# Raw weight buffers of the feed-forward groups dealt out anew: block 22 with two of its own, blocks 11, 21 and 12 in a ring of four

## The chip, the cores and the metric

The kernel runs on one core of a Trainium2 chip. The metric is device time in microseconds (us). The five engines (TensorE for matmuls, VectorE or DVE, ScalarE or ACT, GpSimd or POOL, and SyncE or SP, which issues most transfers) each run their own list of instructions in order and wait for one another through semaphores.

## The reference

A two-layer decoder trunk in float32 on 528 columns (16 meta tokens and 512 tokens): a retention layer and a gated DeltaNet layer, each followed by a SwiGLU feed-forward block. What matters here is the feed-forward block, whose hidden width is 2816:

```python
def swiglu(h, w_gate, w_up, w_down):
    return (jax.nn.silu(h @ w_gate) * (h @ w_up)) @ w_down
...
    for i in range(DEPTH):
        ...
        h = h + mix
        h = h + swiglu(rmsnorm(h, ffn_norm_w[i]), ffn_w_gate[i], ffn_w_up[i], ffn_w_down[i])
```

## The kernel before, in words

**Precision.** Every float32 matmul is made of three: weights and data are each split into a high half (a cast on ScalarE) and a low half (a subtraction on VectorE), and `mm3` (L400 to L407) multiplies high by high, high by low and low by high. A *split* of a raw weight block of 128x1024 (`split_w`, L177) is thus one cast into `whi` (L397) and one subtraction into `wlo` (L398). `whi` and `wlo` have three buffers each, so a cast waits until the matmuls of the third product before have read their weights.

**Hidden half of a feed-forward block** (`ffn_hidden`, L890). The 22 pairs of gate and up tiles are handled two at a time: 11 groups in each layer. For each, `ffn_quad` (L334) fetches four raw blocks of 512 KB, named 11, 21, 22 and 12. The first two groups (`PLAIN`) are done plainly: one row of products with 11 and 12, one with 21 and 22. Beside them the *forms* of the data (`forms`, L191: b11, t1, t2, b22, t3, b21, t4, with their sums in a tile that is also called `wsum`) are made on VectorE and ScalarE. The other nine groups go through `strassen` (L342), which needs seven products of 24 matmuls where the plain way needs eight. In the order of the code they use:

- b11: block 11
- t1: s = 21 + 22 (L374, into the tile `wsum`, of which there is one)
- t2: s = s + 11 (L377)
- b22: s = s + 12 (L380)
- t3: 21 = 11 + 21, written over block 21 (L385)
- b21: block 12
- t4: block 22

Each is split and multiplied, and products add up in the accumulators x, z and y. Between them results are taken out: L364 copies x or z on ScalarE, L368 adds on VectorE, L955 to L961 make silu(gate) times up. The second L364 takes z out after t1, and b22 then adds to z. In layer 0 a matmul of these products has 264 columns, in layer 1 it has 256.

**Raw buffers.** `raw_w` (L174) deals out a ring of `RAW` = 4 buffers, `wraw`, which all weights of the kernel share. In `ffn_quad` blocks 11 and 12 take from that ring; 21 and 22 alternate in two buffers `sraw` of the stage's own pool. A transfer into a buffer waits until the last reader of what it held is done: of 11 that is L377 or L385, of 12 its split after L380, of 21 the split for t3, of 22 the split for t4, the last of the group. SP issues the transfers in its own order, so one that waits holds those behind it.

**The norm at a stage's start.** `row_rsqrt` (L475) sums squares with two kinds of small matmuls (L489, L491), takes the power on GpSimd (L497) and spreads the result with matmuls (L500, L504) in the middle of the first plain row.

**Who sets the order.** The code is written product by product. A list scheduler places the instructions on each engine when the program is built, by its own estimates of when buffers and data are ready, so another dealing of buffers also changes orders. On the chip the order is fixed.

Of the kernel before, what the change touches and what calls it, by code (L numbers as in the profile page):

```python
# [14 lines left out]
P = 128  # L15
# [35 lines left out]
class Hybrid:  # L51
# [282 lines left out]
    def ffn_quad(self, src, sp):  # L334

        raw = {}
        for i, n in enumerate(("11", "21", "22", "12")):
            raw[n] = self.raw_w() if n[0] == "1" else self.t(sp, [P, 1024], "sraw", bufs=2)
            self.nc.sync.dma_start(raw[n], src[i])
        return raw  # L340

# [1433 lines left out]
```

## Time and profile before

| what | us |
|---|---|
| median of 3 runs | 1740.63 (1739.11 to 1741.3) |
| the profiled execution's own time | 1740.59 |
| its span, first to last instruction | 1738.8 |
| TensorE waiting for `wlo` of L398 (all stages) | 5.5 in 13 waits |
| SP holding L339 for a split's subtraction L398 | 198.8 in 45 waits |
| SP holding L339 for L377 | 139.1 in 14 waits |
| layer 0, seven-product groups | 511.69 to 699.20 |
| layer 1, seven-product groups | 1413.71 to 1602.42 |

Times in views are microseconds from the span's start, mean durations of groups are ns. PE is TensorE's matmuls, PEld its weight loads, which run beside matmuls. The end of a matmul is modelled, so the distance from one matmul's start to the next says more than its busy time. "SPq" is SP's queue: a wait there costs nothing unless someone waits for the transfer. The chain of waits follows the work that ended last back to what released it.

### The profile page before, as it was taken

The numbers are of one execution on the slowest core, as the hardware profiler recorded it, in microseconds if no ns is written. First come the engines' busy times: TensorE is split into PE (matmuls) and PEld (weight loads), VectorE is DVE, ScalarE is ACT, GpSimd is POOL, SyncE is SP. The second block draws the span as 40 slices with busy tenths as digits, with TensorE's granted clock in tenths as the row PEclk, the third lists the DMA queues.
The fourth block names the chain that finished last, engine by engine and source line by source line (L and its number), as shares of the span: only waits on it lengthen the run. The fifth ranks groups of instructions, "written<-read, shape, count | busy, mean of one in ns | idle before, by whom it ended". The sixth has DMA issues, their size and how long they took to land.

```text
span 1738.8 us, 30404 instructions
## 1 busy us (share of the span) xinstructions
PE 1696.0 (98%) x12455; PEld 1577.0 (91%) x12455; DVE 1209.5 (70%) x1830; ACT 854.8 (49%) x1524; POOL 75.8 (4%) x130
## 2 busy tenths in 40 slices
PE   9999999899999999999999999999999999999997
PEld 9998989899999999999999978797977889999886
DVE  7868787873497777533688777685858797777322
ACT  5554454553354544422565537665656544445322
POOL 1000000000000000000030000010101000000010
PEclk9999999999999999999999999999999999999999
DMA  6333234472313332333264463332322233333321
GB/s 215 134 97 121 86 108 142 139 246 87 110 62 98 113 107 82 100 89 95 81 209 159 132 180 114 120 113 98 113 96 75 86 97 97 98 99 108 97 97 49
DMA packets 84524, 197.72 MB, mean 114 GB/s; under 512 B 19888, under 2 KB 37472, under 8 KB 83104
## 3 DMA queue, kind: packets, MB, share of 16 engines
q1 hardware_dynamic: 77056, 193.13, 34.2%
q10 hardware_dynamic: 6960, 1.84, 0.5%
q8 instruction: 98, 1.61, 0.4%
q0 software_dynamic: 368, 0.80, 0.1%
q14 instruction: 42, 0.34, 0.1%
HBM read 171.41 MB, written 24.33 MB: 113 GB/s over the span
## 4 chain that ended last, share of the span: by engine, by line
PE 72%; DVE 16%; ACT 5%; DMA 4%; issue 3%; POOL 1%; ACTq 0%; SPq 0%; DVEq 0%; POOLq 0%
PE g L407 53%; PE m L407 13%; DVE wlo L398 5%; ACT whi L397 3%; DMA sraw<-in_w_gu_dram 3%; DVE wraw L264 1%; DVE wsum L380 1%; DVE wsum L377 1%; DVE wsum L374 1%; DMA wraw<-in_w_ret_dram 1%; DVE xlo L530 1%; DVE wlo L171 1%; DVE xhi L398 1%; POOL ss L1435 0%; DMA xhi<-d_sg 0%
## 5 line engine op out<-in xcount | busy, mean ns | idle before, releaser
L171 DVE TENSOR_TENSOR wlo<-wraw,whi 128x1024 fp32r<-128x1024 f32 (+1 forms) x140 | 166.4, 1191 | 177.5 <-ACT whi L170 175.4
L170 ACT CAST whi<-wraw 128x1024 fp32r<-128x1024 f32 (+1 forms) x140 | 143.3, 1024 | 261.8 <-PE g L407 141.3
L407 PE MATMUL g<-fht,whi 128*128 128x264 f32 (+1 forms) x864 | 248.2, 287 | 13.2 <-ACT xlo L291 13.0
L407 PE MATMUL g<-xhi,whi 128*128 128x264 f32 (+1 forms) x1024 | 254.3, 313 | 0.1
L407 PE MATMUL g<-xhi,wlo 128*128 128x264 f32 (+1 forms) x1024 | 247.6, 306 | 2.0 <-DVE wlo L171 2.0
L407 PE MATMUL g<-xlo,whi 128*128 128x264 f32 (+1 forms) x1024 | 247.8, 306 | 0.3 <-DVE xlo L461 0.3
L407 PE MATMUL g<-fht,wlo 128*128 128x264 f32 (+1 forms) x864 | 245.6, 284 | 0.9 <-DVE wlo L398 0.8
L407 PE MATMUL g<-flt,whi 128*128 128x264 f32 (+1 forms) x864 | 245.3, 284 | 0.0
L407 PEld LDWEIGHTS g<-fht,whi 128*128 128x128 f32 x864 | 163.0, 189 | 14.0 <-ACT xlo L291 13.6
L407 PEld LDWEIGHTS g<-xhi,whi 128*128 128x128 f32 x1024 | 165.9, 189 | 10.7 <-issue 0.7
L407 PEld LDWEIGHTS g<-xhi,wlo 128*128 128x128 f32 x1024 | 165.9, 189 | 10.6 <-DVE wlo L171 2.2
L407 PEld LDWEIGHTS g<-xlo,whi 128*128 128x128 f32 x1024 | 166.2, 189 | 7.5 <-DVE xlo L461 0.7
L407 PEld LDWEIGHTS g<-fht,wlo 128*128 128x128 f32 x864 | 162.7, 188 | 1.7 <-DVE wlo L398 1.6
L407 PEld LDWEIGHTS g<-flt,whi 128*128 128x128 f32 x864 | 163.2, 189 | 0.0
L397 ACT CAST whi<-wraw 128x1024 fp32r<-128x1024 f32 x107 | 111.9, 1049 | 97.7 <-issue 36.6
L398 DVE TENSOR_TENSOR wlo<-wraw,whi 128x1024 fp32r<-128x1024 f32 x107 | 129.9, 1220 | 25.8 <-ACT whi L397 25.7
L407 PE MATMUL g<-fhb,wlo 128*128 128x264 f32 (+1 forms) x432 | 124.1, 287 | 4.8 <-DVE wlo L398 4.7
L407 PE MATMUL g<-fhb,whi 128*128 128x264 f32 (+1 forms) x432 | 123.2, 285 | 0.0
L407 PE MATMUL g<-flb,whi 128*128 128x264 f32 (+1 forms) x432 | 122.4, 283 | 0.0
L397 ACT CAST whi<-wsum 128x1024 fp32r<-128x1024 f32 x54 | 56.7, 1050 | 79.8 <-DVE wsum L377 46.7
L398 DVE TENSOR_TENSOR wlo<-wsum,whi 128x1024 fp32r<-128x1024 f32 x54 | 66.0, 1222 | 40.4 <-ACT whi L397 40.4
L407 PEld LDWEIGHTS g<-fhb,wlo 128*128 128x128 f32 x432 | 81.2, 188 | 7.5 <-DVE wlo L398 7.4
(454 smaller groups left out, 3955.6 us busy)
## 6 DMA issues: line engine op xcount, KB each, us to landing
wraw<-in_w_ret_dram SPq DMA_DIRECT2D x56, 512.0 KB, 3.4
wraw<-in_w_gu_dram SPq DMA_DIRECT2D x44, 512.0 KB, 3.4
sraw<-in_w_gu_dram SPq DMA_DIRECT2D x44, 512.0 KB, 3.4
wraw<-in_w_d_dram SPq DMA_DIRECT2D x38, 512.0 KB, 3.5
wraw<-in_w_ro_dram SPq DMA_DIRECT2D x16, 512.0 KB, 3.9
wraw<-in_w_dqk_dram SPq DMA_DIRECT2D x16, 512.0 KB, 3.3
wraw<-in_w_dv_dram SPq DMA_DIRECT2D x16, 512.0 KB, 3.6
wraw<-in_w_dg_dram SPq DMA_DIRECT2D x16, 512.0 KB, 3.4
```

Of the source, the lines that this page charges most:

```text
L170: nc.scalar.copy(hi[:, c], raw[:, c])
L171: nc.vector.tensor_tensor(lo[:, c], raw[:, c], hi[:, c].bitcast(F32), op=ALU.subtract)
L264: self.nc.vector.tensor_tensor(raw[dst], raw[dst], raw[src], op=ALU.add)
L374: nc.vector.tensor_tensor(s, raw["21"], raw["22"], op=ALU.add)
L377: nc.vector.tensor_tensor(s, s, raw["11"], op=ALU.add)
L380: nc.vector.tensor_tensor(s, s, raw["12"], op=ALU.add)
L397: self.nc.scalar.copy(hi, src)
L398: self.nc.vector.tensor_tensor(lo, src, hi.bitcast(F32), op=ALU.subtract)
L407: mm(o, l, r[which], start=first and n == 0, stop=last and n == 2, **kw)
L530: nc.vector.tensor_tensor(o, x, y, op=op)
```

## The change

```diff
         raw = {}
         for i, n in enumerate(("11", "21", "22", "12")):
-            raw[n] = self.raw_w() if n[0] == "1" else self.t(sp, [P, 1024], "sraw", bufs=2)
+            raw[n] = self.t(sp, [P, 1024], "sraw", bufs=2) if n == "22" else self.raw_w()
             self.nc.sync.dma_start(raw[n], src[i])
         return raw
```

The two `sraw` buffers now hold block 22 of two groups in turn. The ring of four holds 11, 21 and 12, so three of its buffers go to each group; block 21 of a group takes the buffer in which 11 of the group before stood. No transfer, cast, sum or product is added or left out.

The scheduler places the work of a seven-product group otherwise. On VectorE, in the second of the nine groups in layer 0, behind the split for b22 (`wsum_5813` and `5775`, `5779` are this group's sum and blocks 21 and 12; `wsum_6045`, `6005`, `6007`, `6009` the next group's sum and blocks 11, 21, 22):

```order
 L380 TENSOR_TENSOR wsum_5813<-wsum_5813,wraw_5779 128x1024
 L398 TENSOR_TENSOR wlo_5878<-wsum_5813,whi_5877 128x1024
-L398 TENSOR_TENSOR wlo_5912<-sraw_5775,whi_5911 128x1024
+L374 TENSOR_TENSOR wsum_6045<-wraw_6007,sraw_6009 128x1024
+L398 TENSOR_TENSOR wlo_5912<-wraw_5775,whi_5911 128x1024
+L385 TENSOR_TENSOR wraw_6007<-wraw_6005,wraw_6007 128x1024
 L398 TENSOR_TENSOR wlo_5943<-wraw_5779,whi_5942 128x1024
 L368 TENSOR_TENSOR ra_5905<-ra_5905,g_5782 128x528
```

The next group's L374 and L385 moved up among the splits of this one; before, they stood some nine instructions further on, behind the split of the next block 11.

On ScalarE, in the same group, from the copy of x after b11 (`ra_5843`) to the cast of block 12:

```order
 L364 COPY ra_5843<-g_5781 128x528
+L397 CAST whi_5877<-wsum_5813 128x1024
+L397 CAST whi_5911<-wraw_5775 128x1024
 L364 COPY ra_5874<-g_5782 128x528
-L397 CAST whi_5877<-wsum_5813 128x1024
-L397 CAST whi_5911<-sraw_5775 128x1024
 L397 CAST whi_5942<-wraw_5779 128x1024
```

The casts for b22 and t3 moved ahead of the copy of z.

SP's queue at the same place (11, 21, 22 and 12 of a group are 6005, 6007, 6009 and 6011; 5775 and 5777 are 21 and 22 of the group before, 6237 is 11 of the next):

```order
 L339 DMA wraw_6005<-in_w_gu_dram 128x1024
-L339 DMA sraw_5775<-in_w_gu_dram 128x1024
+L339 DMA sraw_6009<-in_w_gu_dram 128x1024
+L339 DMA wraw_6007<-in_w_gu_dram 128x1024
 L339 DMA wraw_6011<-in_w_gu_dram 128x1024
-L339 DMA sraw_5777<-in_w_gu_dram 128x1024
 L339 DMA wraw_6237<-in_w_gu_dram 128x1024
```

Before, 21 and 22 of a group came behind 11 of the next group and later; now a group's four blocks stand together, 22 ahead of 21.

At the start of layer 1's feed-forward block, in its first plain row, TensorE has this (`x` is the normed data, `am` and `acc` the sums of squares):

```order
 L407 MATMUL g_15338<-xlo_15067,whi_15330 128x512
 L407 MATMUL g_15338<-xhi_15066,wlo_15331 128x512
-L489 MATMUL m_15365<-ones_76,am_15354 96x1
-L491 MATMUL m_15365<-ones_76,acc_15068 128x1 x4
 L407 MATMUL g_15338<-xhi_15066,whi_15330 128x512
 L407 MATMUL g_15338<-xlo_15067,whi_15330 128x512
 L407 MATMUL g_15338<-xhi_15066,wlo_15331 128x512
+L489 MATMUL m_15365<-ones_76,am_15354 96x1
+L491 MATMUL m_15365<-ones_76,acc_15068 128x1 x4
```

The row-sum matmuls moved back by three matmuls; L500 and L504 keep their place. VectorE's order there, with the split of the first block 21 (`wlo_15420`):

```order
 L473 TENSOR_TENSOR acc_15068<-acc_15068,ra_15261 128x528
 L1510 TENSOR_TENSOR h_73<-h_73,g_15270 128x512 x2
+L398 TENSOR_TENSOR wlo_15420<-wraw_15324,whi_15419 128x1024
 L461 SCALAR_TENSOR_TENSOR xlo_15067<-h_73,ffnw_452,xhi_15066 128x528
 L473 TENSOR_TENSOR acc_15068<-acc_15068,ra_15298 128x528
```

Before, that subtraction stood behind the copy into `am` (L481), five instructions further on. In layer 0 the same split moved ahead of the last norm step, and TensorE's order is the same as before.

## The prediction

> **What bounds the kernel now.** I read the page first: the busy shares, then the chain that ended last.
>
> ```profile
> span 1738.8 us, 30404 instructions
> PE 1696.0 (98%) x12455; PEld 1577.0 (91%) x12455; DVE 1209.5 (70%) x1830; ACT 854.8 (49%) x1524; POOL 75.8 (4%) x130
> ...
> PE g L407 53%; PE m L407 13%; DVE wlo L398 5%; ACT whi L397 3%; DMA sraw<-in_w_gu_dram 3%; DVE wraw L264 1%; DVE wsum L380 1%; DVE wsum L377 1%; DVE wsum L374 1%; DMA wraw<-in_w_ret_dram 1%; DVE xlo L530 1%; DVE wlo L171 1%; DVE xhi L398 1%; POOL ss L1435 0%; DMA xhi<-d_sg 0%
> ```
>
> TensorE is the bound, so a change can give only what TensorE loses. But the chain has 3% (some 45 us) on transfers into `sraw`, the buffers that are dealt out anew. That is no 45 us to win: most of it lies beside matmuls. So next I cut both feed-forward stages into their nine seven-product groups, from the first matmul of one to that of the next. The columns are the stretch, its length, then the busy time and count of TensorE, its weight loads, VectorE, ScalarE and GpSimd, the clock and the DMA.
>
> ```profile
> 574.48:595.00 20.52, 20.52 (x171) 20.52 (x169) 16.44 (x20) 10.23 (x14) 0.00 (x0) 1.00 0.32 103
> ...
> 657.22:678.56 21.34, 20.88 (x170) 20.58 (x169) 17.19 (x21) 10.54 (x15) 0.00 (x0) 1.00 0.32 100
> ...
> sum 187.51, PE 186.02 PEld 184.82 DVE 148.44 ACT 92.73 POOL 0.00; mean PE 20.67 PEld 20.54 DVE 16.49 ACT 10.30 POOL 0.00
> ```
>
> ```profile
> 1413.71:1435.49 21.78, 20.67 (x169) 20.25 (x168) 18.37 (x23) 11.01 (x15) 0.00 (x0) 1.00 0.31 98
> 1435.49:1455.86 20.37, 20.37 (x170) 20.21 (x169) 16.03 (x19) 10.22 (x14) 0.00 (x0) 1.00 0.32 104
> ...
> sum 188.71, PE 184.57 PEld 182.11 DVE 149.39 ACT 92.42 POOL 0.00; mean PE 20.51 PEld 20.23 DVE 16.60 ACT 10.27 POOL 0.00
> ```
>
> Groups of identical work take 20.5 us or 21.3 us. In layer 0 an undisturbed group takes 20.51 to 20.52 us, so nine should take 9 x 20.51 = 184.59; they take 187.51: **2.92 us lost**. In layer 1 no group is clean, so I take the floor from one product in the chain:
>
> ```profile
> 1429.89 2.88 PE m L407 x24
> ```
>
> Seven of these are 20.16 us, nine are 181.44 against 188.71: **7.27 us lost**, of which 21.78 - 20.16 = 1.62 in the first group. All 10.2 us are what any change to these groups could give.
>
> Then the chain within one slow group, in order of time (start, duration, what):
>
> ```profile
> 628.41 1.23 DVE wlo L398
> 629.64 0.03 DVE xlo L961
> 629.66 4.15 DMA sraw<-in_w_gu_dram
> ...
> 633.90 1.23 DVE wsum L374
> ...
> 644.39 1.24 DVE wlo L398
> 645.62 0.04 issue
> 645.67 2.83 PE g L407 x21
> ...
> 650.86 4.30 DMA sraw<-in_w_gu_dram
> ```
>
> This is a loop. The split of block 22, last of its group (628.41), frees its buffer; the next group's 22 can only then be fetched (4.15 us); L374 adds it to 21; L377 and L380 go on adding in the same `wsum`, each between two splits; the split of the fourth sum (644.39) is late for the b22 product, and TensorE waits there. Through the products the loop comes back to the next split of 22. Its turn is 650.86 - 629.66 = 21.20 us, longer than the 20.51 us of matmuls: where it turns, it sets the pace.
>
> **The change part by part.** Block 22 alone rotates through two `sraw` buffers; 11, 21 and 12 take three slots a group in the ring of four. Nothing computed is added or removed: the same 88 transfers of 512 KB, the same casts, subtractions and sums.
>
> *Block 22 (removes the wait).* Its transfer for the next group now waits for the split of 22 of the group before the current one, a whole group (20 us) earlier than L374 needs it. The DMA step falls out of the loop. Gain: at most 2.92 + 7.27.
>
> *Block 21 (a new wait).* Its slot is the one that 11 of the group before held, free when L377 has read it. So its transfer now starts at L377, and L374 of the next group stands in VectorE's order right behind the fourth split of the current one. Is that late? An undisturbed group has these splits and sums, and the view of the tile `sraw` the second fence (engines idle until a transfer landed: us, times; then all landings):
>
> ```profile
> 617.13 1.21 DVE L377 TENSOR_TENSOR wsum<-wsum,wraw 128x1024 f32<-128x1024 f32 x1
> ...
> 623.20 1.22 DVE L398 TENSOR_TENSOR wlo<-wsum,whi 128x1024 fp32r<-128x1024 f32 x1 [1.20 <-ACT whi L397]
> 624.34 1.22 DVE L398 TENSOR_TENSOR wlo<-sraw,whi 128x1024 fp32r<-128x1024 f32 x1
> ```
>
> ```profile
>   DMA sraw<-in_w_gu_dram: 7.3, 13
> ...
> DMA to landing us min/median/max: 3.1/3.4/4.6
> ```
>
> L377 ends at 618.34, the fourth split at 624.42: 6.08 us, and L377, cast, subtraction, L380, cast, subtraction must follow each other, so it can hardly shrink. A transfer lands 3.1 to 4.6 us after issue: 1.4 us to spare at the worst. I cost it at nothing. Behind the waiting L374 would stand the splits of 21 (624.34) and 12. Blocks 12 and 11 are refetched after the splits of 21 and 12, more than half a group before their use; SP issues in the same order in which buffers come free, so no fetch stands behind a later one.
>
> *VectorE's order.* L374 and L385 (1.22 us each) leave the stretch ahead of the t1 split and stand among the splits of the group before. So L377, and all that follows it, comes about 2 us sooner; the b22 split, which now just makes it, is ready some 1.5 us ahead. The split of 21 starts one L374 later, about 625.5 instead of 624.34, and ends at 626.7; its product begins near 627.3. VectorE has 16.4 us of work in 20.5, so it keeps up.
>
> *ScalarE's order.* Before, the b22 cast stands behind the second copy L364, which takes z out before b22 adds to it:
>
> ```profile
> 621.62 0.60 ACT L364 COPY ra<-g 128x528 f32<-128x528 f32 x1 [1.64 <-PE g L407]
> 622.11 1.05 ACT L397 CAST whi<-wsum 128x1024 fp32r<-128x1024 f32 x1
> ```
>
> Now the casts for b22 and t3 stand ahead of that copy. With L377 2 us earlier, cast t2, subtraction, L380 and two casts (about 1.05 + 1.22 + 1.22 + 2 x 1.05), then the copy of 0.6, end about 1 us before b22. I cost this at nothing; if that cover goes, b22 waits for the copy.
>
> *First group of layer 1 (stays).* VectorE works 18.37 of its 21.78 us, the rest of the plain tiles with it, and its order up to the b22 split is unchanged. So 1.62 us stay; bounds 0 and 1.62 of gain, I take 0.
>
> *Start of each stage.* Block 21's first split is moved ahead of the last norm steps. In layer 1 the row-sum matmuls L489 move three matmuls back. VectorE's rows, then GpSimd's power and the weight load that waits for it:
>
> ```profile
> 1366.89 1.28 DVE L1510 TENSOR_TENSOR h<-h,g 128x512 f32<-128x512 f32 x2 [0.58 <-PE g L407]
> 1368.39 0.77 DVE L461 SCALAR_TENSOR_TENSOR xlo<-h,ffnw,xhi 128x528 fp32r<-128x528 f32 x1 [0.21 <-ACT xhi L460]
> ...
> 1371.11 0.19 DVE L481 COPY am<-acc 128x48 f32<-128x48 f32 x1
> ```
>
> ```profile
> 1373.06 1.18 POOL L497 TENSOR_TENSOR rc<-rc,mhalf 128x5 f32<-128x5 f32 x1 [30.60 <-DVE rc L496]
> ```
>
> ```profile
> 1376.26 0.29 PEld L500 LDWEIGHTS m<-ident,rc 16*128 16x128 f32 x2 [0.37 <-issue]
> ```
>
> L461 can start at 1368.17 - 0.08 + 1.14 = 1369.23 behind the inserted subtraction, 0.84 later than now, and `am` with it; three 512-wide matmuls are 3 x 0.24 = 0.72. The power's result reaches TensorE 3.2 us after 1373.06, and L500 already stands 0.37 us waiting for it, so the delay falls on TensorE in full: **+0.84 us** (bounds 0 and 1.2, one whole subtraction). In layer 0 the matmuls keep their place: I take 0, and 0.84 as the bound. The first 22 is now fetched behind the second 12, some 3 us later; it is needed a row of products later: 0.
>
> *Sum.* 2.92 + (7.27 - 1.62) = 8.57 saved, 0.84 lost: 7.73. The profiled execution took 1740.59 us (span 1738.8 and 1.8 around it), the median is 1740.63. 1740.6 - 7.7 = **1732.9 us**.
>
> [...] By the busy shares of matmuls alone, the idle time in the same seventeen groups is 1.49 + (188.71 - 21.78) - (184.57 - 20.67) = 4.52 us; by weight loads it is 2.69 + 166.93 - 161.86 = 7.76; by the pitch of groups 8.57. [...]
>
> **The rivals.**
> *Another wait takes over (0.14).* For: L377 to b22 stays a chain of six steps, and in layer 1 even the best group loses 20.37 - 20.16 = 0.21 us. Against: two sums leave the chain. If 0.21 stays in each of 17 groups, 3.6 us come back: 1736.5.
> *The loss was never the transfer's (0.10).* For: engines sat idle for these transfers only 7.3 us in 13 waits (0.56 each), and undisturbed groups have the same buffers. Then VectorE's sequence sets the turn, and the time is 1740.6 + 0.8 = 1741.4, not faster. Against: L374 leaves that sequence too.
> *Slower: L374 blocks VectorE (0.06).* L374 stands ahead of the split of 21. If 21 lands over 6.08 us after L377, everything behind is late by the excess; 626.7 against 627.5 (the third matmul of the product, the first to read the low half) leaves 0.8, so it decides from 6.9 us. A landing of 8 us would cost 1.2 us in each of 16 groups, 19 us: 1752. Against: 4.6 is the longest landing here. [...]
>
> **How the numbers follow.** Forecast 0.70, at 1732.9, by itself 1730.4 (first group and stage start come free too) to 1735. The range takes in the rival at 1736.5: 1730.0 to 1737.0; what is left out is the 0.10 and the 0.06. A measurement of this kernel tells about 0.2% (3.5 us) from no change, so faster means under 1737.1. The forecast and two thirds of the first rival: 0.79 faster; the rest of it and the second: 0.15 the same; 0.06 slower.
>
> **What would show it.** Right: all groups but layer 1's first at 20.5 and 20.2 to 20.3 us; the `sraw` transfers gone from the chain; no L374 wait on a transfer; the transfer of 21 issued right behind L377; L500's wait 0.8 us longer in layer 1. Wrong: gaps ahead of b22 on ScalarE's L364, gaps ahead of t3 with L374 waiting, or group lengths still at 21.

## The result and the profile after

| | before | after |
|---|---|---|
| median us | 1740.97 (4 runs, 1739.11 to 1743.44) | 1730.32 (4 runs, 1729.1 to 1732.23) |
| profiled execution, its span | 1740.59, 1738.8 | 1732.23, 1730.5 |
| nine groups of layer 0 | 187.51 | 184.37 |
| nine groups of layer 1 | 188.71 | 183.06 |

The ratio is 0.9939, with a 95% interval of 0.9922 to 0.9956. The forecast was 1732.9 us, in a range of 1730.0 to 1737.0, and faster: the time fell inside it, 2.6 us below the forecast.

The page of the changed kernel: its span and busy times, then the chain that ended last, by engine and by line.

```profile
span 1730.5 us, 30404 instructions
PE 1692.9 (98%) x12455; PEld 1576.7 (91%) x12455; DVE 1211.8 (70%) x1830; ACT 857.1 (50%) x1524; POOL 75.8 (4%) x130
...
PE g L407 64%; PE m L407 13%; DVE wlo L398 2%; DVE wraw L264 1%; DMA wraw<-in_w_ret_dram 1%; DVE xlo L530 1%; ACT whi L397 1%; DVE xhi L398 1%; DVE wlo L171 1%; PE m L504 1%; POOL ss L1435 0%; DVE ra L1022 0%; PE m L491 0%; PE m L1171 0%; PE m L1347 0%
```

The transfers into `sraw` (3% of the chain before) are gone from it, and L374, L377 and L380 (1% each) are no longer among its lines; what they held is now matmuls (64% against 53%). The cut of the two stages into their groups, in the same columns as before (stretch, length, busy time and count of each engine, clock, DMA), layer 0 first:

```profile
510.58:531.06 20.48, 20.48 (x170) 20.48 (x169) 18.45 (x23) 10.47 (x14) 0.00 (x0) 1.00 0.31 104
531.06:551.55 20.49, 20.49 (x171) 20.49 (x169) 16.67 (x20) 10.31 (x14) 0.00 (x0) 1.00 0.32 104
...
sum 184.37, PE 184.37 PEld 184.37 DVE 150.04 ACT 93.72 POOL 0.00; mean PE 20.49 PEld 20.49 DVE 16.67 ACT 10.41 POOL 0.00
```

```profile
1411.00:1432.78 21.78, 20.67 (x169) 20.25 (x168) 19.65 (x25) 11.21 (x15) 0.00 (x0) 1.00 0.31 98
1432.78:1452.94 20.16, 20.16 (x170) 20.16 (x169) 16.57 (x20) 10.24 (x14) 0.00 (x0) 1.00 0.32 105
...
sum 183.06, PE 181.95 PEld 181.53 DVE 150.35 ACT 93.72 POOL 0.00; mean PE 20.22 PEld 20.17 DVE 16.71 ACT 10.41 POOL 0.00
```

In seventeen of eighteen groups TensorE's busy time now equals the length: the profile shows no gap there any more. Only layer 1's first group keeps its 21.78 us. Set against before, the profiled execution lost 1.11 us ahead of the first group (511.69 to 510.58), 3.14 in layer 0's groups, gained 1.54 between the stages (714.51 us before, 716.05 now) and lost 5.65 in layer 1's groups: -8.36 us in all, and 1740.59 - 1732.23 is 8.36. So the groups carry 8.79 us; the other two terms are taken up below.

VectorE in one group of layer 0 (from 613.01), the rows that answer to those shown of before:

```profile
612.78 1.22 DVE L377 TENSOR_TENSOR wsum<-wsum,wraw 128x1024 f32<-128x1024 f32 x1
...
618.82 1.22 DVE L398 TENSOR_TENSOR wlo<-wsum,whi 128x1024 fp32r<-128x1024 f32 x1 [1.17 <-ACT whi L397]
620.08 1.22 DVE L374 TENSOR_TENSOR wsum<-wraw,sraw 128x1024 f32<-128x1024 f32 x1
621.22 1.22 DVE L398 TENSOR_TENSOR wlo<-wraw,whi 128x1024 fp32r<-128x1024 f32 x1
```

The next group's L374 starts without a wait, 13 us ahead of its group. The split for b22 ends at 620.04, 7.03 us into the group; in the undisturbed group of before it ended at 624.42, 8.91 us into it.

### The profile page after: what moved, and what is told of

Same layout as the page of the kernel before. It is cut to its first block, busy times and chain, and to the rows that moved or that the text cites. A ratio compares the mean times of both kernels' runs of the same rounds, so it can differ in the third digit from the quotient of the medians.

```text
span 1730.5 us, 30404 instructions
## 1 busy us (share of the span) xinstructions
PE 1692.9 (98%) x12455; PEld 1576.7 (91%) x12455; DVE 1211.8 (70%) x1830; ACT 857.1 (50%) x1524; POOL 75.8 (4%) x130
## 4 chain that ended last, share of the span: by engine, by line
PE 81%; DVE 9%; issue 5%; ACT 2%; DMA 1%; POOL 1%; SPq 0%; POOLq 0%; ACTq 0%; DVEq 0%
PE g L407 64%; PE m L407 13%; DVE wlo L398 2%; DVE wraw L264 1%; DMA wraw<-in_w_ret_dram 1%; DVE xlo L530 1%; ACT whi L397 1%; DVE xhi L398 1%; DVE wlo L171 1%; PE m L504 1%; POOL ss L1435 0%; DVE ra L1022 0%; PE m L491 0%; PE m L1171 0%; PE m L1347 0%
## 5 line engine op out<-in xcount | busy, mean ns | idle before, releaser
L397 ACT CAST whi<-wraw 128x1024 fp32r<-128x1024 f32 x129 | 135.1, 1050 | 122.2 <-issue 55.2
L398 DVE TENSOR_TENSOR wlo<-wraw,whi 128x1024 fp32r<-128x1024 f32 x129 | 156.6, 1219 | 28.3 <-ACT whi L397 28.1
```

What stands on the lines that cost most here:

```text
L397: self.nc.scalar.copy(hi, src)
L398: self.nc.vector.tensor_tensor(lo, src, hi.bitcast(F32), op=ALU.subtract)
```

## The experiments

Where the loss comes from had two candidates that the change moves together: the **transfer** of block 22 behind the last split, and the **place of L374** on VectorE, which the scheduler moved up once the transfer was early. The first runs below take them apart. Each run was timed between runs of the kernel before.

### The change once more

> The changed kernel once more, for the size of the gain and for which parts of a profile come back. If the groups carry the gain, the nine seven-product groups take 184.4 us in layer 0 and 183.1 us in layer 1 again (187.51 and 188.71 before), the first group of layer 1 again 21.78 us, and the median lies at 1729 to 1732 us, 8 to 11 us under the kernel before. If the half-clock stretch that the first profile of this kernel has at 1048.8 us belongs to the change, it stands there again; if it is an accident of one execution, it is gone or elsewhere, and then the profiled time falls by up to 3 us.

Measured: 1730.24 us (1729.24 to 1732.58), ratio 0.9945 (0.9932 to 0.9957). The groups take 184.38 and 183.06 us, to 0.01 us what they took the first time, and layer 1's first again 21.78; the stretch between the stages is 714.5 us, as before the change. The gain is that of the groups; the 1.54 us were of one execution.

### Transfer early, L374 late

```diff
-        s = self.t(sp, [P, 6 * hw], "wsum")[:, :1024]
+        s = self.t(sp, [P, 6 * hw], "wsum")[:, :1024]; nc.vector.tensor_copy(s[:, 0:1], self.c11[:, 1, 0:1]) if self.c11 is not None else None
...
-        out(0, 0, c11[:, 0, :], c11[:, 1, :])
+        out(0, 0, c11[:, 0, :], c11[:, 1, :]); self.c11 = c11
```

(`self.c11` is None ahead of a stage's first group.)

> The new dealing of buffers, but the first sum of a group (L374) can't run ahead: a copy of one column (128x1) into its tile, from a block that the group before finishes late, holds it behind L368 where it stood before the change. So the early transfer stays and the new VectorE order goes. If the transfer is what the loop lacked, the groups stay at 20.5 us and 20.2 us and the time is 1730 to 1734 us (16 copies add under 2 us of VectorE time, beside matmuls). If the earlier place of L374 and L385 brought the gain, the groups go back to 20.8 and 20.9 us on average and the time to 1738 to 1741 us.

Measured: 1743.82 us (1743.3 to 1748.72), ratio 1.0022 (1.0011 to 1.0034): the whole gain is gone, and a little more. VectorE around the start of the group at 615.60, and that group's length:

```profile
613.75 0.15 DVE L373 COPY wsum<-ra 128x1 f32<-128x1 f32 x1
613.93 1.22 DVE L374 TENSOR_TENSOR wsum<-wraw,sraw 128x1024 f32<-128x1024 f32 x1
...
623.97 1.23 DVE L398 TENSOR_TENSOR wlo<-wsum,whi 128x1024 fp32r<-128x1024 f32 x1 [1.17 <-ACT whi L397]
```

```profile
615.60:636.80 21.20, 20.74 (x170) 20.52 (x169) 16.94 (x21) 10.10 (x15) 0.00 (x0) 1.00 0.34 100
```

L374 waits for no transfer here, in no group. It starts 1.67 us ahead of its group, behind both adds of L368, L961 and the copy, and the split for b22 ends at 625.20, 9.60 us into the group. The sixteen groups behind the first of each layer are long, 21.2 us in layer 0 and 20.95 to 21.01 in layer 1. So an early transfer does not bring the gain when L374 stands this late. The run does not show an early transfer with L374 in the place that it had before (between the two adds, 2.81 us ahead of an undisturbed group): the hold put it 1.14 us behind that place, of which the copy is 0.2.

What decides can now be read from both kernels. A slow group of before, at 657.22 (21.34 us):

```profile
655.25 1.22 DVE L374 TENSOR_TENSOR wsum<-sraw,sraw 128x1024 f32<-128x1024 f32 x1 [0.76 <-DMA sraw<-in_w_gu_dram]
...
665.73 1.22 DVE L398 TENSOR_TENSOR wlo<-wsum,whi 128x1024 fp32r<-128x1024 f32 x1 [1.17 <-ACT whi L397]
```

Here L374 did wait for the transfer, 0.76 us, and the split for b22 ends at 666.95, 9.73 us into its group. Against the undisturbed group (8.91, length 20.52) it is 0.82 later and the group 0.82 longer; the held group is 0.69 later and 0.68 longer. The group pays for the lateness of that split, whatever made it late.

The kernel before also shows what the wait itself costs. The wait of L374 and the length of its group, in layer 0 (the group above follows this one), then in layer 1:

```profile
633.90 1.23 DVE L374 TENSOR_TENSOR wsum<-sraw,sraw 128x1024 f32<-128x1024 f32 x1 [0.61 <-DMA sraw<-in_w_gu_dram]
```

```profile
636.03:657.22 21.19, 20.73 (x170) 20.53 (x169) 16.33 (x20) 10.00 (x15) 0.00 (x0) 1.00 0.32 100
```

```profile
1579.31 1.23 DVE L374 TENSOR_TENSOR wsum<-sraw,sraw 128x1024 f32<-128x1024 f32 x1 [0.92 <-DMA sraw<-in_w_gu_dram]
```

```profile
1581.05:1602.42 21.37, 20.70 (x170) 20.29 (x169) 17.19 (x22) 11.20 (x17) 0.00 (x0) 1.00 0.23 75
```

Length less wait is 20.58 us in the group above and in this one of layer 0, and 20.45 in the one of layer 1. In all eleven groups whose L374 waited it is 20.56 to 20.58 in layer 0 and 20.44 to 20.46 in layer 1: each wait went into its group in full.

### Transfer later: block 22 fetched twice

```diff
-            self.nc.sync.dma_start(raw[n], src[i])
+            for _ in range(2 if n == "22" else 1): self.nc.sync.dma_start(raw[n], src[i])
```

> The kernel before, with block 22 fetched twice into the same buffer, one transfer behind the other: in each group the fetch behind the split of 22 takes one landing longer, 3.4 to 4.2 us. If the loop of split, fetch, L374, L377, L380 and late split sets the pace, its turn of 21.20 us becomes 24.6 to 25.4 us in sixteen group-to-group turns (eight in each layer), 3.8 to 4.6 us over the mean of the groups before: 60 to 74 us more, 1800 to 1815 us. If the second transfer overlaps the first, half of that: 1770. If the loss was never the transfer's, the second fetch lies beside other work: 1741 to 1745 us.

Measured: 1788.66 us (1786.75 to 1792.36), ratio 1.0283 (1.0267 to 1.0298): 47.6 us more. The view of L374, what VectorE idled for ahead of it (us, times), in the kernel before, and with the doubled fetch:

```profile
  DMA sraw<-in_w_gu_dram: 6.0, 11
```

```profile
  DMA sraw<-in_w_gu_dram: 44.7, 16
```

The waits stand in all sixteen turns, and the groups grow from 376.2 to 422.1 us. The loop through the transfer is real, and no other work hides it. The size was over-estimated: I added a whole landing to every turn, 60 to 74 us, but the scheduler gave this run another order, in which both adds of L368 and L961 stand ahead of L374 and go through during the fetch; the loop's way from L374 to L377 is 3.87 us here (603.23 to 607.10), where the slow group that the prediction follows has 4.53. So 2.9 us a turn came out of it, not 3.8 to 4.6.

The same edit on the changed kernel:

> The changed kernel with the same doubling: block 22 fetched twice into its buffer, one transfer behind the other. The same edit cost the kernel before 47.6 us. If block 22's transfer is off the loop, with a whole group (20 us) to land, the second landing of 3.4 to 4.2 us lies beside matmuls in all sixteen turns, L374 stays 13 us ahead of its group and the groups stay at 20.49 and 20.16 us: 1730 to 1733 us. If the doubled traffic on SP's queue holds back block 21, which stands behind 22 in the queue and has 6 us from L377 to the fourth split, L374 waits for it by up to 3 us, and own_12 has shown that a wait of 1.5 us of an L374 that stands early costs no group more than 0.5 us: 1731 to 1738 us. If traffic as such costs, tens of us as in the kernel before.

Measured: 1732.34 us (1729.39 to 1735.16), ratio 0.9953 (0.9937 to 0.9969). L374 waits for no transfer, and the groups keep their length: nine in layer 0, then eight in layer 1 behind the first:

```profile
509.04:693.45 184.41, 184.41 (x1515) 184.41 (x1514) 150.01 (x174) 93.75 (x129) 0.00 (x0) 1.00 0.37 120
1430.31:1591.58 161.27, 161.27 (x1346) 161.27 (x1345) 130.72 (x152) 82.55 (x114) 0.00 (x0) 1.00 0.38 123
```

What cost 45.9 us in the groups of before costs nothing in these seventeen (layer 1's first took 0.4 us more). The bytes moved in them rose from 100 and 102 GB/s (the same stretches of the changed kernel) to 120 and 123, so traffic as such is not what hurts.

### A transfer that L374 waits for, early in the group before

```diff
-            raw[n] = self.t(sp, [P, 1024], "sraw", bufs=2) if n == "22" else self.raw_w()
+            raw[n] = self.t(sp, [P, 1024], "sraw", bufs=2) if n == "12" else self.raw_w()
```

> Another dealing: block 12 alone has two buffers, 11, 21 and 22 share the ring, so 22 of a group takes the buffer of 21 of the group before and its transfer starts behind the split for t3, about 3 us earlier than before the change. L374 of the next group stands ahead of the split of 22 (t4) on VectorE. By the loop, what counts is the turn: one round of VectorE's in-order list is 16.4 us of work plus 2 to 3 us held at L374 until 22 has landed, 19 us, under the 20.5 us of matmuls; VectorE runs ahead by that much and no group loses: 1730 to 1734 us. By the rival that a late L374 blocks VectorE, the split for t4 behind it comes 1.2 to 2.0 us too late for its product in each of sixteen groups: 1750 to 1762 us. If only a 22 that is fetched a whole group ahead cures the loss, the time is 1738 to 1741 us.

Measured: 1738.05 us (1733.75 to 1740.53), ratio 0.9983 (0.9974 to 0.9992). The view of L374, then one of its waits in the group at 612.99:

```profile
  DMA wraw<-in_w_gu_dram: 8.1, 8
```

```profile
625.02 1.23 DVE L374 TENSOR_TENSOR wsum<-wraw,wraw 128x1024 f32<-128x1024 f32 x1 [0.81 <-DMA wraw<-in_w_gu_dram]
626.16 0.70 DVE L368 TENSOR_TENSOR ra<-ra,g 128x528 f32<-128x528 f32 x1
626.77 1.22 DVE L398 TENSOR_TENSOR wlo<-wraw,whi 128x1024 fp32r<-128x1024 f32 x1
```

VectorE waits longer for transfers than it did before the change (8.1 us against 6.0), with splits queued behind the waiting L374. Yet the groups lose only 1.0 us in layer 0 (185.34 against 184.37), where all eight waits are, and 0.4 in layer 1, all of it in the first group. The rival "a late L374 blocks VectorE" had asked for 1.2 us and more in every group. It is there, but small: the five groups with waits of up to 1.15 us lose at most 0.02, the three with the longest, 1.17, 1.38 and 1.55 us, lose 0.11, 0.33 and 0.50. The sum itself is in time: the wait shown ends 8 us before the group that needs it.

The median is nevertheless 7.8 us above the changed kernel, and the groups hold 1.4 of that. Another 5.1 come at the start of layer 1's feed-forward block. The chain of waits at its row sums, and the stretches around them (lengths and columns as above):

```profile
1367.47 0.20 DVE am L481
1367.67 0.14 issue
1367.81 0.30 PE m L489 x2
```

```profile
1366.00:1368.00 2.00, 0.19 (x3) 0.22 (x3) 1.63 (x4) 1.53 (x3) 0.00 (x0) 1.00 0.69 277
1368.00:1370.00 2.00, 2.00 (x13) 1.91 (x13) 1.34 (x3) 0.88 (x1) 0.00 (x0) 0.75 0.00 0
1370.00:1372.00 2.00, 2.00 (x6) 1.52 (x6) 1.24 (x3) 0.00 (x0) 1.81 (x1) 0.50 0.75 262
1372.00:1374.00 2.00, 2.00 (x6) 1.61 (x5) 0.00 (x0) 0.00 (x0) 0.28 (x1) 0.50 0.74 246
1374.00:1376.00 2.00, 2.00 (x6) 1.52 (x6) 0.00 (x0) 0.00 (x0) 0.00 (x0) 0.55 0.04 16
```

The scheduler put L489 so far ahead in TensorE's order that it stands waiting for `am` (1.8 us without a matmul); behind it the granted clock is half for 6.8 us. From the first matmul of the stage to the first seven-product group it is 52.18 us, where the changed kernel has 47.07. This is a side effect of the order, in another place than the buffers.

### One layer alone, and the mirror

One layer alone, with `self.l1 = lo > 0` set in `ffn_hidden`:

```diff
-            raw[n] = self.t(sp, [P, 1024], "sraw", bufs=2) if n == "22" else self.raw_w()
+            raw[n] = self.t(sp, [P, 1024], "sraw", bufs=2) if n == "22" and self.l1 or not self.l1 and n[0] == "2" else self.raw_w()
```

> The change in layer 1 alone; layer 0 keeps the old dealing. By the groups, layer 0 loses 2.9 us again (187.5 us for nine) and layer 1 takes 183.06 us: 1740.9 less 5.65, 1735.3 us. TensorE's order at the start of layer 1's feed-forward block is that of the changed kernel, with the row-sum matmuls L489 three matmuls back; if that costs the 0.84 us that I gave it, the distance from L461's last norm step to the first seven-product group is 0.84 us longer than before and the time is 1736.1; if it costs nothing, 1735.3.

Measured: 1734.49 us (1732.78 to 1737.9), ratio 0.9967 (0.9955 to 0.9979). Layer 0's groups take 187.87 us and layer 1's 183.06: layer 1's gain does not hang on layer 0's dealing.

The mirror has `n == "21"` in the condition in place of `n == "22"`.

> The mirror: block 21 alone has two buffers, and 11, 22 and 12 share the ring, so that 22 of a group takes the buffer of 11 of the group before, free after L377. VectorE's order in the groups is that of the changed kernel (L374 right behind the fourth split), and TensorE's order at the start of layer 1's block is that of the kernel before (L489 not moved). If what counts is that neither operand of L374 waits for the last split of the group before, the groups take 20.49 and 20.16 us and the time is 1729 to 1732 us, as with the change; the two then tell by their difference what the moved L489 costs: up to 0.84 us less here if that step was right, no difference (within 0.2 us in the stretch of the trace) if it was not. If it must be 22 that has its own buffers, 1738 to 1741 us.

Measured: 1730.19 us (1729.51 to 1731.7), ratio 0.9942 (0.9929 to 0.9954), the same as the change. It is not block 22 that must have its own buffers. It is enough that neither operand of L374 waits for the last split of the group before (VectorE's order in the groups is that of the change here too). The stretch from the first matmul of layer 1's block to its first seven-product group, in the kernel before, after, and in the mirror (with L489 where it was):

```profile
1366.69:1413.71 47.02, 47.02 (x213) 38.24 (x212) 41.95 (x68) 23.30 (x34) 1.18 (x1) 1.00 0.27 90
```

```profile
1363.93:1411.00 47.07, 47.07 (x213) 38.16 (x212) 41.77 (x68) 23.17 (x34) 1.17 (x1) 1.00 0.27 90
```

```profile
1363.50:1410.48 46.98, 46.98 (x213) 38.21 (x212) 41.86 (x68) 23.28 (x34) 1.18 (x1) 1.00 0.28 90
```

The moved L489 costs 0.05 to 0.09 us: the stretch is 47.07 or 47.08 us in every profile in which it is moved as in the changed kernel (seven), 46.98 to 47.02 in the three in which it is not (own_12 aside).

### What is left in layer 1's first group

Two tries at its 1.62 us. The first deals the forms out faster in layer 1 (`pause=FORM - (lo > 0)` in the call of `forms`).

> The changed kernel, with the forms of layer 1's data dealt out every two ticks instead of three, so that VectorE makes them earlier in the plain tiles. The first seven-product group of layer 1 still takes 21.78 us, 1.62 over the others: its L377 starts 3.14 us behind the group's start where the other groups have -0.18, and the split for b22 ends at 10.35 us, 1.5 us behind the latest that costs nothing (8.85). If VectorE's backlog from the forms is what makes it late, the forms end earlier, L377 comes forward by 1.5 us or more, and up to 1.62 us go: 1728.6 to 1730 us. If the backlog is the plain tiles' own results (L939, L941), which wait for TensorE, nothing changes: 1730 us.

Measured: 1730.09 us (1729.89 to 1732.23), ratio 0.9944 (0.9931 to 0.9956); the group takes 21.79 us. VectorE's rows there in the changed kernel say why:

```profile
1411.20 1.29 DVE L939 TENSOR_TENSOR ra<-g,rb 128x512 f32<-128x512 f32 x2
1412.40 1.22 DVE L398 TENSOR_TENSOR wlo<-wsum,whi 128x1024 fp32r<-128x1024 f32 x1
1413.54 0.68 DVE L941 TENSOR_TENSOR ra<-ra,ra 128x512 f32<-128x512 f32 x1
1414.14 1.22 DVE L377 TENSOR_TENSOR wsum<-wsum,wraw 128x1024 f32<-128x1024 f32 x1
```

No form stands there any more. L939 takes the last plain product out, which ends as the group begins (1411.00), and the sums queue behind it in order; with the forms done sooner VectorE only idles ahead of L939 (0.24 us in that run). The second try moves L941 and the subtraction behind it to GpSimd:

```diff
-                nc.vector.tensor_tensor(tt[0], tt[0], tt[1], op=ALU.mult)
-                self.split(hi[:, j, :], low[:, j, :], tt[0])
+                e = nc.gpsimd if lo and j == PLAIN - 1 else nc.vector; e.tensor_tensor(tt[0], tt[0], tt[1], op=ALU.mult)
+                nc.scalar.copy(hi[:, j, :], tt[0]); e.tensor_tensor(low[:, j, :], tt[0], hi[:, j, :].bitcast(F32), op=ALU.subtract)
```

> The changed kernel, with the last product and the last subtraction of the plain tiles of layer 1 (L941 and L942, 128x512) on GpSimd instead of VectorE, where they stand between the sums of the first seven-product group. If the group's 1.62 us come from VectorE's order there, L377 starts 0.69 us sooner and the subtraction behind it goes too, so the split for t2 starts as soon as its cast is done; the split for b22 ends near 9.7 us instead of 10.35 and the group takes 20.9 to 21.1 us instead of 21.78: 1729.5 us. If the two copies out of the last plain product (L939), which wait for TensorE, are what hold the chain, only the 0.69 us come or nothing. If GpSimd slows VectorE's own instructions while it works, the group stays at 21.8 us or gets longer.

Measured: 1731.36 us (1729.85 to 1734.27), ratio 0.9942 (0.9928 to 0.9955); the group takes 22.27 us, 0.5 more. GpSimd, then VectorE at the same time:

```profile
1414.28 2.06 POOL L941 TENSOR_TENSOR ra<-ra,ra 128x512 f32<-128x512 f32 x1 [40.48 <-ACT ra L940]
```

```profile
1413.97 1.22 DVE L398 TENSOR_TENSOR wlo<-wsum,whi 128x1024 fp32r<-128x1024 f32 x1
1415.22 2.19 DVE L377 TENSOR_TENSOR wsum<-wsum,wraw 128x1024 f32<-128x1024 f32 x1
```

L377 starts sooner, as wanted, but takes 2.19 us in place of 1.22: it ends 1.07 us after GpSimd's multiplication does (1416.34). No run here beat the changed kernel by more than the measurement can tell.

## Why the prediction held, step by step

- **The loss in the groups** (2.92 and 7.27 us, 8.57 to be had): 8.79 came. The floors were right to 0.03 us a group. Of the measures that the prediction weighed, the pitch of groups (8.57) came nearest, the idle time by weight loads (7.76) was 12% short, and that by matmul busy time (4.52) half. Matmul busy time counts part of the loss as work here: 20.88 us in the group at 657.22, where the same work at 574.48 took 20.52 from start to start.
- **Block 22** (the DMA step falls out of the loop): right. L374 waits for no transfer, and a doubled fetch costs 45.9 us in the groups of before and none in seventeen of after.
- **VectorE's order**: right in its size (L377 started 1.62 us into an undisturbed group, 617.13 - 615.51, and now 0.23 us ahead of it, 612.78 - 613.01: 1.85 us sooner, about 2 forecast; the b22 split 1.88 us sooner, some 1.5 forecast), but I gave it no price of its own and put the whole 8.57 to the transfer. The held run shows that the place matters: with L374 1.14 us behind its old place the early transfer is worth nothing. What the old place costs without a wait is read from the kernel before. Its eleven waits are 6.0 us together and went into their groups in full, so of the 8.8 us some 6.0 came from the transfer and some 2.8 from the old order. The five groups behind the first in which L374 did not wait point the same way: they are 0.02, 0.03, 0.03 and 0.15 us longer than after in layer 0 and 0.21 in layer 1. This split is an estimate from rows; no run had the old order without the waits.
- **Block 21's new wait** (0): right. Its transfer is issued at 614.07, right behind L377, and lands 3.2 us later; L374 comes at 620.08, so 2.8 us were to spare.
- **ScalarE's order** (0): right, no product waits for L364 (none did before).
- **First group of layer 1 stays** (0 of 1.62): right, 21.78 again, and two tries did not shorten it.
- **Start of layer 1** (+0.84 us): wrong. It cost 0.05. I read the 0.37 us that L500 stands as a wait for GpSimd's power, so that a later `am` would fall on TensorE in full. Here are L489 and L500 after:

```profile
1369.49 0.24 PEld L489 LDWEIGHTS m<-ones,am 128*96 128x96 f32 x2 [0.26 <-issue]
```

```profile
1373.55 0.29 PEld L500 LDWEIGHTS m<-ident,rc 16*128 16x128 f32 x2 [0.37 <-issue]
```

  The distance from L489 to L500 shrank from 4.85 to 4.06 us, and L500's 0.37 stayed to the digit. `am` and L489 did come 0.83 and 0.84 us later (L489 4.72 us into the stage before, 5.56 now), but L500 only 0.05 (9.57 and 9.62). GpSimd's power had ended 2.0 us ahead of L500 before, 1.3 us now and 6.0 us in own_12, each time with the same 0.37: it is no wait for the power, and the delay ends in that room. A constant idle time that does not move with its supposed releaser is no sign of one. The step whose size was off is this term of the sum; it hid part of the gain.
- **The sum**: -7.73 forecast, -8.79 + 0.05 = -8.74 measured by the steps. The median fell by 10.65. The rest is outside the change's places: the first group starts 1.1 us sooner after, but over all profiled runs it starts between 509.0 and 511.7 us, and it is open whether any of that is the change's. So 1.9 us of the fall are explained by no step, and the time lies just above the low end of the range (1730.0).

Of the rivals, "another wait takes over" asked for 0.21 us in each of 17 groups; none is left, all but the first stand at 20.16 us; by the estimate above that rest went with the place of L374. "Never the transfer" falls with the doubled fetch and with the waits that lengthen their groups one for one. "L374 blocks VectorE" needed landings of over 6.9 us, and no L374 of the changed kernel waited; own_12 shows the mechanism with waits long enough (1.38 and 1.55 us cost 0.33 and 0.50 there).

## What to carry to other kernels

When a buffer's last reader sits at the end of a turn and its next content at the head of a chain in the following turn, free it earlier: which tile has the private buffers matters less than which reader frees them. Then look where the in-order engine has the head of that chain: an early transfer pays in full only if the instruction that uses it does not stand late in that order (held back to 1.14 us behind its old place, it cost the groups 12.2 us against the changed kernel, more than the 8.8 that the kernel before had lost). And measure a suspected lateness at the point where the bottleneck needs the data (here the end of one split after the group's start); it priced waits and orders alike, to 0.01 us in the two groups worked out above.

## What the runs showed of the hardware

**A VectorE sum took longer beside a GpSimd multiplication.** In pool_row L377 took 2.19 us beside a GpSimd multiplication of 128x512 (1414.28 to 1416.34), and 1.22 in the changed kernel (at 1414.14), where GpSimd does nothing in that group. The split that was already running when the multiplication began (1413.97 to 1415.19) kept its 1.22, and L377 ended 1.07 us after GpSimd did. What made L377 longer is not shown. It is one instance, and times on GpSimd are rough.

**Half-clock stretches come and go between executions.** The first profile of the changed kernel has one that the kernel before lacks:

```profile
1045.00:1048.00 3.00, 3.00 (x33) 2.27 (x31) 1.82 (x3) 1.69 (x6) 0.10 (x1) 1.00 0.91 359
1048.00:1051.00 3.00, 3.00 (x11) 1.92 (x11) 1.39 (x2) 2.14 (x7) 0.00 (x0) 0.64 0.05 15
1051.00:1054.00 3.00, 3.00 (x13) 2.35 (x12) 0.76 (x2) 2.42 (x6) 0.00 (x0) 0.50 0.00 0
```

Here TensorE runs without a gap that the profile shows, and its clock is half from 1048.8 us on, for 6.8 us. The kernel before has one of 3.4 us at 1342 instead, which this execution lacks; the repeat had one of 3.4 us at 1050. From one gap in TensorE's work to the next around 1050 us it is 58.2 us without a stretch there, 59.6 with the short one and 61.1 with the long one, so a single profile of this kernel can't be read closer than these 1.4 to 2.9 us without lining up its stretches.

**Half-clock stretches stand behind some gaps of 1.3 and 1.8 us.** In own_12 the clock fell to 0.50 within 1.2 us of a gap of 1.82 us without a matmul. A gap of 1.3 us stands 23 to 24 us ahead of layer 1's feed-forward block in all eleven profiles; a half-clock stretch follows within 1.1 us in six of them, in the other five none. That the gap is the cause is not shown: the stretch at 1048.8 us has no gap in the 13 us ahead of it, and no run here varied the gap alone.
